# A two-layer decoder trunk on one core: a place of its own for turned weights, and a new order of the projection's pieces

## The chip, the core and the metric

The kernel runs on one core of a Trainium2 chip. The metric is the device time of one launch in microseconds, the median of several runs; lower is better. One further execution was taken by the hardware profiler, and all durations below come from it.

## What is computed

Two layers act on a residual stream x of 256 rows and 1024 columns, all in float32. Each normalises x, multiplies it with one wide input projection, runs three groups of heads, gates them and projects back:

```python
for layer in range(DEPTH):                                   # 2
    h = rms_norm(x, norm_g[layer])
    proj = jnp.einsum('btd,dc->btc', h, w_in[layer])         # 1024 -> 3584 columns
    sb_q, sb_k, sb_v, sb_g, mb_q, mb_k, mb_v, mb_g, mem_q, mem_g = jnp.split(proj, split_at, axis=-1)
    o_sb  = merge_heads(stick_breaking_attention(sb_q, sb_k, sb_v)) * silu(sb_g)      # 6 heads of 64
    o_mb  = merge_heads(moba_attention(rotary(mb_q), rotary(mb_k), mb_v)) * silu(mb_g)  # 6 heads
    m = rms_norm(mem, mem_norm_g[layer])                     # 256 memory rows
    mk, mv = jnp.split(jnp.einsum('bmd,dc->bmc', m, w_mem_kv[layer]), 2, axis=-1)
    o_mem = merge_heads(memory_attention(mem_q, mk, mv)) * silu(mem_g)                # 4 heads
    x = x + jnp.einsum('btc,cd->btd', jnp.concatenate([o_sb, o_mb, o_mem], -1), w_out[layer])
return rms_norm(x, final_norm_g)
```

With 256 rows the second group (mb) is plain causal softmax attention. The stick-breaking group (sb) replaces the softmax by a chain of log-sigmoids and a running sum over later keys.

## The kernel before

**Pieces and chunks.** The input projection is cut into pieces by head group and purpose: sb_q, sb_k, sb_v, sb_g, mb_q, mb_k, mb_v and mb_g have 384 columns, mem_q, mem_g, mk and mv 256; in layer 0 the first two are one piece, sb_qk. After them come three pieces of the output projection, wo0, wo1 (384 columns) and wo2 (256). The table `ORDER` (L45) gives the order of the pieces in each layer. A piece's weights are loaded in chunks of up to 128 x 768 floats (several of the eight k blocks side by side) into five `raw` tiles. The very first chunk is split into two halves.

**Two halves of each number.** A chunk is rounded to `hi` (ScalarE or VectorE, L395), VectorE subtracts to get `lo` (L404), and then the raw tile's next load is issued on SP's queue (`dma_chunk`, L377). Seven hi and lo pairs exist (`LEAD`). The activations are split in the same way. A product is three matmuls per k block: hi by hi, hi by lo, lo by hi. A "T" piece (queries, keys and gates; `tr_unit`, L492) comes out turned, with the weights as the stationary operand. An "N" piece (values, the rotated mb queries and keys, the output projection; `nat_unit`, L483) comes out with rows on the partitions.

**Heads.** Heads are handled in pairs. For sb, `sb_head` (L646) and `pair_sums` (L673) compute the scores, a chain of ScalarE and VectorE steps, two kinds of running sums on TensorE, and the weights `wT` (four tiles, held until the pair's product). For mb and mem, `soft_head` (L687) computes the softmax weights `w` with queries on the partitions; a condition on `turn["w"]` lets a pair start only when at most one pair before it has not been turned, the three mb pairs first and the two memory pairs behind them. These weights have to be turned before they can multiply the values. `pair_turn` (L711) does that: VectorE turns 32 x 32 blocks into a staging tile D (L723), SP writes D to a DRAM tile Z (L729), and four more SP issues read Z back into a tile F with the blocks in their places (L737). Three tiles D are there, and F is taken from the same three. `pair_task` (L745) multiplies F with the values (L775), frees F, multiplies with the gate and makes `mxhi` and `mxlo`, the output projection's input. Sb feeds its k blocks 0 to 2, mb 3 to 5, mem 6 and 7.

**The output projection** (L1057) first does k 0 to 5 of wo0 and wo1, then k 6 and 7 of both, then all of wo2. `resid_task` adds the result to x. In layer 0 `norm_task` then makes the next layer's input.

**Two activation buffers.** `Ts` (L285) has two of them, of 128 x 8 x 512. In a layer one holds the normalised rows (hT) and the other the normalised memory rows (mT); they change places from layer to layer. mT is read by mk and mv only.

**A planner writes the order.** The kernel is emitted by a list scheduler (`Sched`, L78). Every step of every task names its engine, its needs and its buffers, and has a cost by formula; the scheduler keeps a clock for each engine and emits the step that could start first, by priority among those close together. The order on each engine's queue is fixed by this. What the planner thinks of a DMA counts in it: a load is ready at the end of a byte queue `dma_t` at 380 GB/s plus 2200 ns (L326), and a trip to DRAM or back takes `DMA_LAT`, 3000 ns, plus its bytes at 300 GB/s, outside that byte queue (L731, L740).

**Start.** SP issues the first half chunk, the gain columns gc, the second half chunk and then xT blocks and chunks in turn; xT's first block is on ScalarE's queue (L426 to L433). In layer 0 the memory rows are loaded at the second piece (`MEM_AT`). Those for layer 1 are scaled into hT (L1023, L1049) when only mk or mv is left in layer 0's order, or after its last piece.

Of the kernel before, what the change touches and what calls it, by code (L numbers as in the profile page):

```python
# [7 lines left out]
F32 = mybir.dt.float32  # L8
# [8 lines left out]
D = 1024  # L17
# [22 lines left out]
X1_AT = 8  # L40
DMA_GBS = 380.0
SP_ISSUE = 450.0
DMA_LAT = 3000.0
MEM_AT = 1
ORDER = (["sb_qk", "mb_q", "sb_g", "mem_q", "mb_k", "mk", "mb_g", "sb_v", "mb_v", "mem_g", "mv"],  # L45
         ["mk", "mv", "sb_k", "mb_q", "mb_k", "sb_q", "mem_q", "sb_v", "sb_g", "mb_g", "mb_v", "mem_g"])
GATES = {"sb_g": ((0, 1, 2),), "mb_g": ((0, 1, 2),), "mem_g": ((0,), (1,))}
HOLD = 4000.0
SPARE2 = 2
# [146 lines left out]
def hybrid_trunk(ctx: ExitStack, tc: tile.TileContext, x, mem, norm_g, w_in, w_mem_kv, w_out,  # L196
# [73 lines left out]
    def sb(name, shape, dt=F32):  # L270
        return cpool.tile(shape, dt, name=name)
# [26 lines left out]
    S.res["a"] = Res([sb(f"a{i}", [128, 384]) for i in range(3)])  # L298
    S.res["w"] = Res([sb(f"w{i}", [128, 512]) for i in range(4)])
    S.res["ah"] = Res([(sb(f"ah{i}", [128, 384], FR), sb(f"al{i}", [128, 384], FR)) for i in range(2)])  # L300
    S.res["wT"] = Res([sb(f"wT{i}", [128, 384]) for i in range(4)])
    S.res["D"] = Res([sb(f"D{i}", [128, 1024]) for i in range(3)])
    dpool = ctx.enter_context(tc.tile_pool(name="turn", bufs=1, space=bass.MemoryType.DRAM))
    S.res["Z"] = Res([dpool.tile([128, 1024], F32, name=f"Z{i}") for i in range(3)])
    S.res["ga"] = Res([sb(f"ga{i}", [128, 768]) for i in range(2)])
# [12 lines left out]

    dma_t = {"t": 500.0}

    def dma(dst, src, name=None, q=None, now=0.0):
        (q or nc.sync).dma_start(dst, src)  # L322
        if q is None:
            S.T["sp"] = max(S.T["sp"], now) + SP_ISSUE
        n = _free(dst) * 4 * dst.shape[0]
        dma_t["t"] = max(dma_t["t"], now) + n / DMA_GBS  # L326
        if name:
            S.ready[name] = dma_t["t"] + 2200.0


    class Piece:
# [42 lines left out]
                chunks.append((p, kk, c, half))  # L374
    prog = {"dma": 0, "hi": 0, "lo": 0, "cur": 0}

    def dma_chunk(now=0.0):  # L377
        j = prog["dma"]
        if j >= len(chunks):
            return  # L380
        p, kk, c, w = chunks[j]
        n = len(kk)
        dma(raws[j % RAW][:, :n * w].rearrange("p (k c) -> p k c", c=w),
            p.src[:, kk[0]:kk[0] + n, c:c + w], ("raw", j), now=now)
        prog["dma"] += 1
        if j == X67_AT:
            load_xT(6, 8, now=now)
        for t, at in enumerate((X0_AT, X1_AT)):
            if j == at:
                dma(xs[:, t, :], x_r[:, t, :], ("x", t), now=now)  # L390
        if j == CST_AT:
            dma(cst, consts[:, 0:512], "cst", now=now)
            dma(S.res["w"].items[0][2][:, :256], consts[:, 512:768], "msk", now=now)
# [29 lines left out]
        for k in range(k0 + 1, k1):  # L423
            S.ready["xT", k] = S.ready["xT", k0]

    dma_chunk()  # L426
    load_xT(0, 1, nc.scalar)
    dma(gc, gcols, "gc")
    dma_chunk()
    for k in range(1, 4):  # L430
        load_xT(k, k + 1)
# [254 lines left out]

    def soft_head(l, h, kind):  # L687
        mb = kind == "mb"
        reg = [(0, 128), (128, 384)] if mb else [(0, 256), (256, 512)]
        _, (st,) = yield R("dve", alloc=["st"], need=[("qkdone", l, kind, h)])  # L690
        sc = scs.pop((l, kind, h))
        for t, (r0, r1) in enumerate(reg):
            nc.vector.tensor_reduce(st[:, t:t + 1], sc[:, r0:r1], axis=AX.X, op=OP.max, negate=True)  # L693
            S.op("dve", 1.0417 * (r1 - r0) + 65.0)
            if t == 0:
                yield R("dve")
        _, (w,) = yield R("act", alloc=["w"], cond=lambda: 5 * l + (0 if mb else 3) + h // 2 <= turn["w"] + 1)
        for t, (r0, r1) in enumerate(reg):
            act(w[:, r0:r1], sc[:, r0:r1], AF.Exp, bias=st[:, t:t + 1], accum_out=st[:, 2 + t:3 + t])
        S.free("bank", sc)  # L700
        yield R("dve")
        nc.vector.reciprocal(st[:, 0:2], st[:, 2:4])
        S.op("dve", 81.0)
        yield R("dve")
        for t, (r0, r1) in enumerate(reg):
            ts(w[:, r0:r1], w[:, r0:r1], st[:, t:t + 1])
        S.free("st", st)
        S.mark(("w", l, kind, h))
        ws[l, kind, h] = w

    def pair_turn(l, kind, c):  # L711


        n = 3 if kind == "mb" else 4
        e = 64 * n
        D = None
        for b in range(2):
            h = 2 * c + b
            _, bufs = yield R("dve", need=[("w", l, kind, h)], alloc=[] if b else ["D"])
            D = D or bufs[0]  # L720
            w = ws.pop((l, kind, h))
            o = D[:, :4 * e].rearrange("p (j m r) -> p m j r", j=4, r=32)[:, b * n:(b + 1) * n]
            nc.vector.transpose(o, w[:, :n * 128].rearrange("p (m j r) -> p m j r", j=4, r=32))  # L723
            S.op("dve", 1.0417 * n * 128 + 65.0)
            S.free("w", w)
        turn["w"] += 1
        _, (Z,) = yield R("sp", alloc=["Z"])
        Zv = Z[:, :4 * e]
        nc.sync.dma_start(Zv, D[:, :4 * e])  # L729
        S.op("sp", SP_ISSUE)  # L730
        t = S.cur.t + DMA_LAT + 512 * e * 4 / 300.0  # L731
        S.res["D"].items.append((t, None, D))
        S.ready["dump", l, kind, c] = t
        _, (F,) = yield R("sp", need=[("dump", l, kind, c)], alloc=["D"])
        Fv = F[:, :4 * e].rearrange("p (i e) -> p i e", i=4)
        for j in range(4):
            nc.sync.dma_start(Fv[32 * j:32 * j + 32],  # L737
                              Zv.rearrange("(i r) (j e) -> j r i e", i=4, j=4)[j])
            S.op("sp", SP_ISSUE)
        t = S.cur.t + DMA_LAT + 512 * e * 4 / 300.0  # L740
        S.res["Z"].items.append((t, None, Z))
        S.ready["F", l, kind, c] = t
        Fs[l, kind, c] = F

    def pair_task(l, kind, c):  # L745
# [30 lines left out]
        if kind == "sb":  # L776
            for wT in w2:
                S.free("wT", wT)
        else:
            S.free("D", F)  # L780
        S.mark(("pv", l, kind, c))
        _, (m,) = yield R("dve", need=[("g", l, k)], alloc=["ev"])
        tt(m, o[:, :256], gT[:, k, :], OP.mult)
# [132 lines left out]
    def main():  # L916
# [16 lines left out]
            scale_task(uT, ("memT", 0), 16, mT, ("mT", 0), P_M0)  # L933
            S.spawn(rows_task(3, lambda t: gb, "mem", "rm", rcm, rbm), P_RM)

        late = []

        def late_mem():
            yield R("sp", need=[("qkdone", 0, "mb", h) for h in range(6)])
# [3 lines left out]
        for l in range(DEPTH):  # L943
# [75 lines left out]
            for i, p in enumerate(ORDER[l]):  # L1019
# [13 lines left out]
                elif p in ("sb_v", "mb_v"):  # L1033
                    yield from N_piece(p, hT, hneed, lambda t, acc: evac_v(l, p, t, acc, rr_(t), 6, "rx"))
                elif p == "mem_q":
                    yield from T_piece(p, hT, 2, hneed,
                                       lambda c, acc: evac_T(l, "mem_q", c, acc, 0.125, rb, "rx"))
                elif p == "mb_q":
                    yield from N_piece(p, hT, hneed, lambda t, acc: rope_task(
                        l, "mb_q", t, acc, rr_(t, True) if l == 0 else 0.125))  # L1040
                elif p == "mb_k":
                    yield from N_piece(p, hT, hneed, lambda t, acc: rope_task(
                        l, "mb_k", t, acc, rr_(t) if l == 0 else 1.0))
                elif p in GATES:
                    yield from T_piece(p, hT, sum(map(len, GATES[p])), hneed, lambda c, acc: gate_evac(
                        l, p[:-2], c, acc, [g for g in GATES[p] if c in g][0]))

# [76 lines left out]
```

## Time and profile before

| | |
|---|---|
| median of 3 runs | 291.1 us (290.92 to 292.39) |
| the profiled execution | 292.06 us, of which the span from first to last instruction is 290.2 |
| mean granted TensorE clock | 0.990 |
| DMA | 58.94 MB, mean 203 GB/s; weight loads mostly 384 KB each, 4.3 to 4.4 us from issue to landing (median) |
| splitting the weights | VectorE's lo 101.8 us (111 instructions), ScalarE's hi 82.4 us (103) |

How to read it: an engine's row gives its busy microseconds, its share of the span and its instructions. PEld is TensorE's loading of stationary operands, beside its matmuls. Behind a row in square brackets stand the idle time of the engine just before it and what ended it. The chain of waits goes back from the last instruction, at each step to what released it. `D<-Z` is the way back of turned weights, `Z<-D` the dump. Tiles carry no buffer numbers, and in the kernel before F is one of the tiles D.

### The profile page before, as it was taken

To read this page: it belongs to the slowest core of one execution; us is meant where nothing else is said; L and a number is where in the kernel's file an instruction comes from. 1 tells how busy PE (TensorE), PEld (TensorE's weight loads), DVE (VectorE), ACT (ScalarE), POOL (GpSimd) and SP (SyncE) were. 2 spreads that over 40 slices of the span, in tenths; PEclk is the share of its full clock that TensorE was granted. 3 is DMA by queue.
4 is the path that set the end of the run, shared out by engine and by line. 5 is a ranking of instruction groups with operands and counts; after the bars stand their busy time and mean duration, and the time that the engine had idled before them with its cause. 6 is when DMAs were issued, how large, how long until landed. Compare 5 with 4: busy or idle time off the path is not lost.

```text
span 290.2 us, 5037 instructions
## 1 busy us (share of the span) xinstructions
PE 275.3 (95%) x1757; PEld 246.0 (85%) x1757; DVE 225.2 (78%) x498; ACT 187.9 (65%) x420; POOL 4.0 (1%) x10
## 2 busy tenths in 40 slices
PE   7899999999999999969999999999999999998991
PEld 4789978998898889957989899988998889887991
DVE  3858799999997999963779467549889999976272
ACT  3979699974597567830766445638969569574052
POOL 0020000000000000000000000000000000000000
PEclk9999999999999999997999999999999999999998
DMA  6998955568679674994286947441684876992003
GB/s 190 396 403 265 365 143 173 151 202 264 185 248 306 213 218 166 283 266 139 61 282 164 308 114 252 116 158 39 184 272 161 241 210 201 308 269 61 0 2 145
DMA packets 43994, 58.94 MB, mean 203 GB/s; under 512 B 3137, under 2 KB 40641, under 8 KB 43969
## 3 DMA queue, kind: packets, MB, share of 16 engines
q1 hardware_dynamic: 43392, 57.24, 63.9%
q0 software_dynamic: 288, 1.05, 1.1%
q8 instruction: 14, 0.23, 0.3%
q10 hardware_dynamic: 288, 0.33, 0.3%
q14 instruction: 12, 0.09, 0.1%
HBM read 53.10 MB, written 5.51 MB: 202 GB/s over the span
## 4 chain that ended last, share of the span: by engine, by line
PE 59%; DMA 19%; DVE 9%; ACT 5%; issue 4%; SPq 2%; DVEq 0%; ACTq 0%
PE bank L226 58%; DMA raw<-in_w_in_dram 8%; DMA D<-Z 7%; DVE lo L248 3%; DMA gb<-in_mem_dram 3%; SPq L322 2%; DMA raw<-in_w_out_dram 2%; ACT hi L242 2%; PE bank L231 1%; DVE T L252 1%; DVE D L723 1%; DVE gT L248 1%; ACT a L244 1%; ACT w L244 1%; ACT junk L244 0%
## 5 line engine op out<-in xcount | busy, mean ns | idle before, releaser
L248 DVE TENSOR_TENSOR lo<-raw,hi 128x768 fp32r<-128x768 f32 (+2 forms) x111 | 101.8, 922 | 15.4 <-ACT hi L242 14.4
L226 PE MATMUL bank<-T,hi 128*128 128x512 f32 (+1 forms) x294 | 100.8, 396 | 1.4 <-ACT hi L242 1.1
L242 ACT CAST hi<-raw 128x768 fp32r<-128x768 f32 (+2 forms) x103 | 82.4, 814 | 23.8 <-PE bank L226 9.7
L226 PE MATMUL bank<-hi,T 128*128 128x384 f32 (+1 forms) x320 | 77.8, 328 | 0.0
L226 PE MATMUL bank<-T,lo 128*128 128x256 f32 x288 | 73.0, 281 | 0.6 <-DVE lo L248 0.6
L226 PEld LDWEIGHTS bank<-T,hi 128*128 128x128 f32 x294 | 53.1, 188 | 12.5 <-ACT hi L242 1.3
L226 PEld LDWEIGHTS bank<-hi,T 128*128 128x128 f32 x320 | 55.8, 189 | 0.8 <-issue 0.5
L226 PEld LDWEIGHTS bank<-T,lo 128*128 128x128 f32 x288 | 53.2, 189 | 3.3 <-DVE lo L248 0.9
L226 PE MATMUL bank<-lo,T 128*128 128x384 f32 (+1 forms) x160 | 51.9, 324 | 0.0
L226 PE MATMUL bank<-hi,mxhi 128*128 128x384 f32 (+1 forms) x96 | 31.0, 323 | 0.0
L226 PE MATMUL bank<-hi,mxlo 128*128 128x384 f32 (+1 forms) x96 | 30.6, 319 | 0.0
L226 PE MATMUL bank<-lo,mxhi 128*128 128x384 f32 (+1 forms) x96 | 30.6, 319 | 0.0
L226 PEld LDWEIGHTS bank<-lo,T 128*128 128x128 f32 x160 | 30.1, 188 | 0.1
L244 ACT ACTIVATE junk<-xs 128x384 bf16<-128x384 f32 (+2 forms) x16 | 8.4, 522 | 21.9 <-DVE xs L248 21.1
L226 PEld LDWEIGHTS bank<-hi,mxhi 128*128 128x128 f32 x96 | 18.4, 191 | 1.3 <-issue 1.3
L226 PEld LDWEIGHTS bank<-hi,mxlo 128*128 128x128 f32 x96 | 18.3, 191 | 0.0
L226 PEld LDWEIGHTS bank<-lo,mxhi 128*128 128x128 f32 x96 | 18.3, 190 | 0.0
L244 ACT ACTIVATE w<-bank,st 128x256 f32<-128x256 f32 (+1 forms) x40 | 17.1, 448 | 0.6 <-DVE st L693 0.6
L693 DVE TENSOR_REDUCE st<-bank 128x1 f32<-128x256 f32 (+1 forms) x40 | 13.1, 376 | 3.8 <-PE bank L226 3.8
L242 ACT COPY gT<-bank 128x256 f32<-128x256 f32 x16 | 5.9, 371 | 15.4 <-PE bank L226 15.2
L244 ACT ACTIVATE ga<-ga 128x768 f32<-128x768 f32 (+1 forms) x24 | 15.3, 636 | 0.9 <-DVE ga L252 0.7
L248 DVE TENSOR_TENSOR xs<-bank,xs 128x384 f32<-128x384 f32 (+1 forms) x12 | 6.1, 512 | 12.5 <-PE bank L226 12.5
(115 smaller groups left out, 319.3 us busy)
## 6 DMA issues: line engine op xcount, KB each, us to landing
raw<-in_w_in_dram SPq DMA_DIRECT2D x71, 384.0 KB, 4.4
raw<-in_w_out_dram SPq DMA_DIRECT2D x20, 384.0 KB, 4.3
raw<-in_w_mem_kv_dram SPq DMA_DIRECT2D x8, 384.0 KB, 3.4
Z<-D SPq DMA_DIRECT2D x6, 384.0 KB, 4.5
D<-Z SPq DMA_DIRECT2D x24, 96.0 KB, 4.1
uT<-memT_dram SPq DMA_DIRECT2D x8, 256.0 KB, 5.1
Z<-D SPq DMA_DIRECT2D x4, 512.0 KB, 3.3
D<-Z SPq DMA_DIRECT2D x16, 128.0 KB, 6.7
```

The source lines that it names most:

```text
L226: nc.tensor.matmul(out, lhsT=lhsT, rhs=rhs, start=start, stop=stop, **kw)
L231: nc.tensor.transpose(out, in_, idt)
L242: nc.scalar.copy(out, in_)
L244: nc.scalar.activation(out, in_, func, **kw)
L248: nc.vector.tensor_tensor(out, a, b, op=op)
L252: nc.vector.scalar_tensor_tensor(out, a, s, b, op0=op0, op1=op1)
L322: (q or nc.sync).dma_start(dst, src)
L693: nc.vector.tensor_reduce(st[:, t:t + 1], sc[:, r0:r1], axis=AX.X, op=OP.max, negate=True)
L723: nc.vector.transpose(o, w[:, :n * 128].rearrange("p (m j r) -> p m j r", j=4, r=32))
```

## The change

- Turned weights come back into tiles of their own, F0 in layer 0 and F1 in layer 1: four places each, quarters of the layer's mT. They are given out once both mk and mv have been emitted in that layer. D has two tiles instead of three and is staging only; wT has five instead of four.
- `ORDER` is new in both layers. In layer 0 mk and mv stand fifth and sixth, mb_k second, mem_g last. In layer 1 the gates sb_g and mb_g come early, and sb_k, sb_v and mb_v are the last three.
- With it, layer 1's memory rows are scaled after the last piece of layer 0, since neither mk nor mv is the last one any more.
- The first half chunk is issued on ScalarE's queue, ahead of xT's first block; gc is the first issue of SP's queue.
- The planner's model of DMAs: loads and trips share one byte queue; runs of up to 1024 bytes count at 300 GB/s, longer ones at 380; a load's latency is 2200 ns as before, a trip's 3000.
- In `soft_head` the name `first` stands for an expression that was there before.

```diff
-DMA_LAT = 3000.0
+DMA_LAT = 2200.0
+DMA_GBS_1K = 300.0
+TRIP_LAT = 3000.0
 MEM_AT = 1
-ORDER = (["sb_qk", "mb_q", "sb_g", "mem_q", "mb_k", "mk", "mb_g", "sb_v", "mb_v", "mem_g", "mv"],
-         ["mk", "mv", "sb_k", "mb_q", "mb_k", "sb_q", "mem_q", "sb_v", "sb_g", "mb_g", "mb_v", "mem_g"])
+ORDER = (["sb_qk", "mb_k", "sb_g", "mb_q", "mk", "mv", "mem_q", "sb_v", "mb_g", "mb_v", "mem_g"],
+         ["mk", "mv", "mb_q", "mb_g", "sb_g", "sb_q", "mb_k", "mem_g", "mem_q", "sb_k", "sb_v", "mb_v"])
...
-    S.res["wT"] = Res([sb(f"wT{i}", [128, 384]) for i in range(4)])
-    S.res["D"] = Res([sb(f"D{i}", [128, 1024]) for i in range(3)])
+    S.res["wT"] = Res([sb(f"wT{i}", [128, 384]) for i in range(5)])
+    S.res["D"] = Res([sb(f"D{i}", [128, 1024]) for i in range(2)])
+    S.res["F0"], S.res["F1"] = Res([]), Res([])
...
+    def queue(nbytes, run, now):
+
+        dma_t["t"] = max(dma_t["t"], now) + nbytes / (DMA_GBS if run > 1024 else DMA_GBS_1K)
+        return dma_t["t"] + DMA_LAT
+
...
-        n = _free(dst) * 4 * dst.shape[0]
-        dma_t["t"] = max(dma_t["t"], now) + n / DMA_GBS
+        t = queue(_free(dst) * 4 * dst.shape[0], dst.shape[-1] * 4, now)
         if name:
-            S.ready[name] = dma_t["t"] + 2200.0
+            S.ready[name] = t
...
-    def dma_chunk(now=0.0):
+    def dma_chunk(now=0.0, q=None):
...
-    dma_chunk()
+    dma(gc, gcols, "gc")
+    dma_chunk(q=nc.scalar)
     load_xT(0, 1, nc.scalar)
-    dma(gc, gcols, "gc")
     dma_chunk()
...
-        t = S.cur.t + DMA_LAT + 512 * e * 4 / 300.0
+        t = queue(2048 * e, 4096, S.cur.t) + TRIP_LAT
         S.res["D"].items.append((t, None, D))
         S.ready["dump", l, kind, c] = t
-        _, (F,) = yield R("sp", need=[("dump", l, kind, c)], alloc=["D"])
+        _, (F,) = yield R("sp", need=[("dump", l, kind, c)], alloc=["F%d" % l])
...
-        t = S.cur.t + DMA_LAT + 512 * e * 4 / 300.0
+        t = queue(2048 * e, 1024, S.cur.t) + TRIP_LAT
...
-            S.free("D", F)
+            S.free("F%d" % l, F)
...
+                if {"mk", "mv"} <= set(ORDER[l][:i + 1]) and not S.res["F%d" % l].items and l not in given:
+                    given.add(l)
+                    for f in range(4):
+                        S.free("F%d" % l, mT[2][:, 2 * f:2 * f + 2, :].rearrange("p k c -> p (k c)").bitcast(F32))
```

More of the change, by code (lines that the diff above doesn't have):

```diff
@@ L383, in dma_chunk @@
         dma(raws[j % RAW][:, :n * w].rearrange("p (k c) -> p k c", c=w),
-            p.src[:, kk[0]:kk[0] + n, c:c + w], ("raw", j), now=now)
+            p.src[:, kk[0]:kk[0] + n, c:c + w], ("raw", j), q, now)
         prog["dma"] += 1
@@ L688, in soft_head @@
         mb = kind == "mb"
+        first = 0 if mb else 3
         reg = [(0, 128), (128, 384)] if mb else [(0, 256), (256, 512)]
@@ L696, in soft_head @@
                 yield R("dve")
-        _, (w,) = yield R("act", alloc=["w"], cond=lambda: 5 * l + (0 if mb else 3) + h // 2 <= turn["w"] + 1)
+        _, (w,) = yield R("act", alloc=["w"], cond=lambda: 5 * l + first + h // 2 <= turn["w"] + 1)
         for t, (r0, r1) in enumerate(reg):
@@ L934, in mem_loads @@
             S.spawn(rows_task(3, lambda t: gb, "mem", "rm", rcm, rbm), P_RM)
-        late = []
+        late, given = [], set()
         def late_mem():
@@ L1043, in main @@
                         l, "mb_k", t, acc, rr_(t) if l == 0 else 1.0))
-                elif p in GATES:
+                if {"mk", "mv"} <= set(ORDER[l][:i + 1]) and not S.res["F%d" % l].items and l not in given:
+                    given.add(l)
+                    for f in range(4):
+                        S.free("F%d" % l, mT[2][:, 2 * f:2 * f + 2, :].rearrange("p k c -> p (k c)").bitcast(F32))
+                if p in GATES:
                     yield from T_piece(p, hT, sum(map(len, GATES[p])), hneed, lambda c, acc: gate_evac(
```

## The prediction, made before the changed kernel was run

> **What bounds the kernel now.** I read the page first, then a table by stage, then TensorE's waits and the chain of waits.
>
> ```profile
> span 290.2 us, 5037 instructions
> ...
> PE 275.3 (95%) x1757; PEld 246.0 (85%) x1757; DVE 225.2 (78%) x498; ACT 187.9 (65%) x420; POOL 4.0 (1%) x10
> ...
> PE 59%; DMA 19%; DVE 9%; ACT 5%; issue 4%; SPq 2%; DVEq 0%; ACTq 0%
> ```
>
> TensorE is busy for 95% of the span and has the largest share of the chain. The change neither adds nor removes a matmul, so it can only fill the holes. The table by stage shows where these are (columns: stretch, its length, PE, PEld, DVE, ACT, POOL, granted clock, DMA share, GB/s):
>
> ```profile
> 0.00:10.00 10.00, 7.40 (x33) 4.55 (x34) 4.15 (x9) 5.06 (x8) 0.41 (x5) 1.00 0.77 242
> 10.00:30.00 20.00, 20.00 (x119) 18.38 (x119) 15.72 (x31) 17.50 (x39) 2.36 (x3) 1.00 0.96 351
> 30.00:118.00 88.00, 86.59 (x574) 76.74 (x573) 81.49 (x203) 65.39 (x159) 0.73 (x1) 1.00 0.70 220
> 118.00:147.00 29.00, 25.83 (x160) 23.93 (x160) 18.66 (x36) 13.70 (x29) 0.00 (x0) 0.94 0.70 180
> 147.00:257.00 110.00, 109.58 (x712) 98.57 (x711) 87.92 (x186) 73.28 (x158) 0.53 (x1) 1.00 0.66 203
> 257.00:284.00 27.00, 25.94 (x169) 23.84 (x168) 15.86 (x35) 11.34 (x27) 0.00 (x0) 1.00 0.23 54
> 284.00:290.20 6.20, 0.01 (x1) 0.00 (x0) 1.40 (x3) 1.62 (x5) 0.00 (x0) 0.80 0.45 169
> ```
>
> The holes are 2.60 us in the head, 0, 1.41 in layer 0's pieces, 3.17 in layer 0's output projection, 0.42 in layer 1's pieces, 1.06 in layer 1's output projection, and 6.2 in the tail, which the change does not touch. VectorE is the second load: 81.49 of 88 us (93%) in layer 0's pieces, 87.92 of 110 (80%) in layer 1's. TensorE's waits name the two holes in the middle:
>
> ```profile
> PE bank L226 <- DMA D<-Z: 4.2, 2, 3.2
> ```
>
> That is the way back of a turned weight pair, and the chain of waits in order of time shows why the first one is late:
>
> ```profile
> 106.30 0.70 DVE D L723
> ...
> 116.76 7.07 DMA D<-Z
> ...
> 123.85 7.14 DMA D<-Z
> ...
> 250.02 0.48 ACT mb_v L242
> ...
> 252.14 0.11 DVE ev L248
> ```
>
> The same on TensorE's and on SP's timeline:
>
> ```profile
> 105.04 2.17 PE L226 MATMUL bank<-D,mb_v 128*64 128x256 f32 x24
> ...
> 126.87 1.08 PE L226 MATMUL bank<-D,mv 128*64 128x256 f32 x8
> 131.12 1.98 PE L226 MATMUL bank<-D,mv 128*64 128x256 f32 x8 [3.17 <-DMA D<-Z]
> 133.03 0.69 PE L226 MATMUL bank<-hi,mxhi 128*128 128x384 f32 x1
> ...
> 134.15 0.36 PE L226 MATMUL bank<-hi,mxhi 128*128 128x384 f32 x1
> ...
> 134.71 0.33 PE L226 MATMUL bank<-hi,mxhi 128*128 128x384 f32 x1
> ...
> 262.91 1.08 PE L226 MATMUL bank<-D,mv 128*64 128x256 f32 x8 [1.06 <-DMA D<-Z]
> ```
>
> ```profile
> 109.36 0.34 SPq L729 DMA_DIRECT2D Z<-D  x1
> ...
> 113.12 0.46 SPq L729 DMA_DIRECT2D Z<-D  x1
> ...
> 115.68 1.98 SPq L737 DMA_DIRECT2D D<-Z  x4
> 118.21 2.96 SPq L322 DMA_DIRECT2D raw<-in_w_out_dram  x3
> 122.27 1.98 SPq L737 DMA_DIRECT2D D<-Z  x4
> ...
> 252.71 5.46 SPq L737 DMA_DIRECT2D D<-Z  x8
> ```
>
> The three D tiles serve twice, as staging of a dump and as the place that it comes back to. The three mb pairs hold all of them until their weights are used, at 105.04. Only then does VectorE turn the first memory head (106.30); the dumps leave at 109.36 and 113.12, the returns at 115.68 and 122.27, the second behind three weight loads, and each takes about 7.1 us to land. The plan had counted on 4.75 (its constants: 3.0 + 524,288 bytes at 300 GB/s), so it placed both memory products too early in TensorE's fixed order.
>
> **The change, part by part.** The working is against the profiled execution: 292.06 us, 1.86 of it around the span. The median of the runs is 291.1, which is 0.96 below; I carry the same difference over.
>
> *Places in the idle memory rows (F0, F1), D from three to two.* Staging no longer waits for mb_v: a D tile is held for one dump. The memory heads of layer 0 can turn as soon as their softmax is done. Five pairs share four places, so the fifth return, memory pair 1, still waits until a first mb pair is used. Call the end of mb_v M. The mb products take 2.17 us (105.04), the issue 1.98, the landing 7.14: with a microsecond of hand-overs the pair is there at about M + 12. It is needed after mem_g, the mb products and those steps of wo0 and wo1 that use no memory head, which are 72 matmuls (two blocks, two row halves, six k, three products). Their rate stands in this stretch of the first of them:
>
> ```profile
> 117.90:126.80 8.90, 8.90 (x53) 8.72 (x51) 7.02 (x12) 5.05 (x9) 0.00 (x0) 1.00 1.09 272
> ```
>
> That is 0.168 us each: 12.1 for the 72, 8.1 for a piece of 48, and, since mem_g has two thirds of such a piece's columns, 5.4 for it. So the pair is needed at M + 5.4 + 2.2 + 12.1 = M + 19.7 in layer 0: 7.7 us of cover. The hole goes whole, and with it the slow restart. The products after the wait took 1.98 instead of 1.08, and the three matmuls from 133.03 took 1.12 against 0.56 for the three from 134.15: 0.90 + 0.56. Gain 3.17 + 0.90 + 0.56 = 4.6. Least gain, if the memory chain moves up by half only: 1.5.
>
> The restart is a matter of the clock: the row for 118 to 147 has a granted 0.94, and the pause of 1.06 at 262.91 left the products at 1.08. The Trainium skill (TensorE: Matmul & The Clock Gate, Part 1: The HAM clock gate) says that the clock halves after an idle window of about 3.4 us and needs as long to come back; an estimate by that page is half of 3.4, 1.7 lost, so 4.9 for this term and a sum of -5.5 below. The trace shows 1.46 lost after a pause of 3.17, so a pause just under the page's window was enough.
>
> *Layer 1's return.* There mb_v is now the last piece, so the fifth pair is there at M + 12 and needed at M + 2.2 + 12.1 = M + 14.3: 2.3 us of cover. Before, both memory returns were issued after 252.71 and cost 1.06. The trip is now planned in the same byte queue as the loads, so the product should be placed later. I take -0.7, between -1.06 (gone) and what rival 1 says.
>
> *mb_v last in layer 1.* From its copy (250.02) to the first product with the gate (252.14) are 2.1 us, and the hi and lo parts follow; 3.2 in all is my estimate. TensorE has the three sb steps of wo0 (9 matmuls, 1.5 us) and the mb products (2.2) meanwhile. +0.3, between 0 and 1.7 (3.2 less the 1.5).
>
> *Memory k, v early; new order.* The matmuls are the same. In layer 0 mk comes 5.4 us sooner (mem_q no longer stands ahead of it) and mv five pieces sooner, and both need the scaled memory rows and their statistics from a VectorE that is 93% busy; the work for layer 1's memory rows moves from before the last piece into the output projection, where VectorE has 18.66 of 29 us. In layer 1 the sb heads move to the end and two gates to the front. VectorE and ScalarE have the same total; layer 1 stood at 80% with 0.42 us lost, layer 0 at 93% with 1.41 lost, so a denser last third is worth about the difference of these, 1 us, at most. I take +0.2, near to nothing, because the totals are unchanged; it lies between -1.8 (1.41 and 0.42 both gone) and rival 2.
>
> *First half chunk on ScalarE's queue.*
>
> ```profile
> 0.74 0.38 SPq L322 DMA_DIRECT2D raw<-in_w_in_dram  x1
> 0.76 0.39 ACTq L322 DMA_DIRECT2D uT<-xT_dram  x1
> ...
> 1.18 0.42 SPq L322 DMA_DIRECT2D gc<-gcols_dram  x1
> ...
> 4.07 0.51 ACT L244 ACTIVATE T<-uT,gc 128x256 fp32r<-128x256 f32 x1 [2.06 <-DMA gc<-gcols_dram]
> ...
> 7.45 0.83 ACT L242 CAST hi<-raw 128x768 fp32r<-128x768 f32 x1 [0.61 <-DMA raw<-in_w_in_dram]
> ...
> 8.33 1.66 PE L226 MATMUL bank<-T,hi 128*128 128x512 f32 x6 [1.14 <-ACT hi L242]
> ```
>
> Each SP issue after the first goes out 0.44 us sooner (1.18 - 0.74). The xT column behind the chunk on ScalarE's queue goes 0.39 later, while gc, for which the first step waited at 4.07, comes 0.44 sooner: the first matmul may slip by up to 0.3. But TensorE waits again at 8.33 for a cast that waited for its chunk, and from there on it is full. So the head is worth what that chunk gains: -0.4, between -0.44 and +0.3.
>
> *The rest* (a fifth wT, the loads at 300 GB/s for short rows): 0. It alters the plan only; matmuls, casts and bytes are the same.
>
> Sum: -0.4 - 4.6 - 0.7 + 0.3 + 0.2 = -5.2. That is 286.9 us for a profiled execution and 291.1 - 5.2 = 285.9 as a median.
>
> **The rivals.**
>
> *1. The fifth pair stalls layer 1 instead.* Its cover is thin (2.3 us), SP's queue put three loads ahead of the second return, and the plan's error for one landing was 2.4 (7.14 against 4.75). If the return again stands behind such loads (from 117.66, where the first four issues end, to 122.27: 4.6 us), the hole is 4.6 - 2.3 = 2.3, and the restart adds between nothing (as after 1.06) and 1.46 (as after 3.17), say 0.8: 3.1 us more than forecast, 289.0. Against it: the weight loads are nearly all out by then (23% DMA share from 257 on).
>
> *2. Layer 1's end is bound by the sb chain: slower.*
>
> ```profile
> 212.90 0.92 PE L226 MATMUL bank<-sb_q,sb_k 64*128 64x256 f32 x8
> ...
> 228.58 0.87 PE L226 MATMUL bank<-wT,sb_v 128*64 128x256 f32 x8
> ```
>
> The last sb pair took 15.7 us from its scores to its product, when the memory and mb softmax shared VectorE. Now it has sb_v and mb_v behind it, 16.2 us, and its result is the first that wo0 uses. More is queued on VectorE then, six sb heads and four memory heads at once. If the chain takes 22.5 us, TensorE stands for 6.3, and the restart adds 1.5: 7.8 less 5.2 is +2.6, 293.7. It makes the kernel slower by over 0.5% from a chain of about 21.4 us on (16.2 + 5.2, with the 1.5 of the restart as the excess). For it: 93% load in layer 0. Against: layer 0 lost only 1.41 at that load.
>
> *3. What goes at the end comes back in layer 0.* mk and mv finish before the memory rows' statistics are there, their four accumulators keep four of the eight banks, and the heads' scores wait for banks. If the 1.41 grows by 4.5, the change is worth -0.7: 290.4. Against it: the mb scores start sooner too, and the third sb pair has a fifth wT.
>
> **How the numbers follow.** Forecast 0.58, rival 1 0.16, rival 3 0.12, rival 2 0.14. Half a per cent is 1.5 us, about what a measurement of this kernel can tell from no change. Faster: the forecast and three quarters of rival 1, 0.70. Same: the rest of rival 1 and most of rival 3, 0.14. Slower: rival 2 and the tail of rival 3, 0.16. The forecast's own bounds are -0.44 - 4.63 - 1.06 + 0 - 1.8 = -7.9 (283.2) and about -1.5 (289.6); with the spread of the runs the low end is 282.6. The high end takes in rivals 1 and 3 and the milder half of rival 2: 292.6.
>
> **What would show it.** Layer 0's output projection without a wait for D<-Z and at clock 1.00, about 24.4 us long instead of 29; memory dumps that leave before the mb products; the matmul of 8.33 near 7.9; a wait of under 0.5 us on the return in layer 1; VectorE at about 85% to 93% in layer 1's last third with TensorE full. A wait of TensorE for mxhi or wT before wo0 in layer 1 would speak for rival 2, one of over 2 us on the return for rival 1, PE idle of over 4 us between 40 and 100 for rival 3. I am wrong if TensorE's holes outside head and tail still sum to 5 us or more.

## The result, and the profile after

The changed kernel takes 282.95 us (282.13 to 284.54 in six runs), the kernel before 291.4 beside it (289.12 to 292.39 in six): a ratio of 0.9719 [0.9675, 0.9763], 8.45 us off where 5.2 were forecast. The forecast's side and range hold; the gain is 1.6 times the forecast, and much of this document is about those 3 us. A ratio here and below compares undisturbed runs alone, so it is not always the quotient of the two medians beside it.

The page of the changed kernel, its span, its load and the chain of waits by engine:

```profile
span 280.5 us, 5046 instructions
...
PE 271.7 (97%) x1757; PEld 245.7 (88%) x1757; DVE 225.0 (80%) x496; ACT 189.8 (68%) x422; POOL 3.9 (1%) x10
...
PE 92%; DMA 3%; DVE 1%; ACT 1%; issue 1%; ACTq 0%
```

The DMA share of the chain fell from 19% to 3%. The span is 9.7 us shorter (290.2 to 280.5): TensorE's idle time fell by 6.1 us (14.9 to 8.8), its busy time by 3.6 for the same 1757 matmuls. Part of that 3.6 is the slow restart of 1.46 (matmuls that ran at half clock behind the hole). The rest is probably pauses too: the profile models the ends of matmuls, so short pauses can hide in them. That is argued, not shown.

The table by stage (columns as in the prediction's) has the same four stretches, moved to where they now begin:

```profile
10.00:114.50 104.50, 104.50 (x684) 94.23 (x684) 96.33 (x227) 81.60 (x186) 2.97 (x4) 1.00 0.82 265
114.50:139.40 24.90, 24.90 (x161) 23.30 (x161) 18.71 (x41) 15.93 (x39) 0.00 (x0) 1.00 0.55 150
139.40:244.70 105.30, 104.78 (x670) 95.06 (x669) 84.50 (x176) 75.27 (x163) 0.53 (x1) 1.00 0.67 205
244.70:274.30 29.60, 29.57 (x210) 27.84 (x208) 19.27 (x43) 9.85 (x23) 0.00 (x0) 1.00 0.24 73
```

The stretch of layer 0's output projection was 29.00 us long with TensorE busy for 25.83 at a granted clock of 0.94; it is now 24.90 long, full, at 1.00. After the head the whole kernel has one hole left. All of TensorE's waits (us in total, times, longest):

```profile
PE bank L228 <- DVE junk L927: 1.2, 1, 1.2
PE bank L228 <- ACT T L246: 0.9, 1, 0.9
PE bank L233 <- DVE w L254: 0.5, 1, 0.5
```

No return of turned weights is among them. TensorE's timeline shows where the memory products (`mv`) now stand, and in the row of 144.05 the hole of 0.52 us (the last row is the last matmul):

```profile
5.24 1.14 PE L228 MATMUL bank<-T,hi 128*128 128x256 f32 x6 [0.88 <-ACT T L246]
...
7.64 1.62 PE L228 MATMUL bank<-T,hi 128*128 128x512 f32 x6
...
107.77 2.17 PE L228 MATMUL bank<-T,mb_v 128*64 128x256 f32 x24
...
114.56 0.34 PE L228 MATMUL bank<-hi,mxhi 128*128 128x384 f32 x1
...
116.76 1.08 PE L228 MATMUL bank<-T,mv 128*64 128x256 f32 x8
...
125.78 1.08 PE L228 MATMUL bank<-T,mv 128*64 128x256 f32 x8
...
139.41 0.40 PE L228 MATMUL bank<-T,hi 128*128 128x512 f32 x1
...
144.05 0.66 PE L233 MATMUL bank<-cst,w 128*128 128x128 f32 x4 [0.52 <-DVE w L254]
...
260.48 1.08 PE L228 MATMUL bank<-T,mv 128*64 128x256 f32 x8
...
273.99 0.28 PE L228 MATMUL bank<-lo,mxhi 128*128 128x256 f32 x1
```

Both products of layer 0 take 1.08, where the late one had taken 1.98. On SP's queue, around them:

```profile
96.10 0.38 SPq L737 DMA_DIRECT2D Z<-D  x1
...
103.28 1.83 SPq L745 DMA_DIRECT2D T<-Z  x4
...
105.86 0.47 SPq L737 DMA_DIRECT2D Z<-D  x1
107.17 8.99 SPq L330 DMA_DIRECT2D raw<-in_w_out_dram  x6
116.25 1.84 SPq L745 DMA_DIRECT2D T<-Z  x4
```

Both memory dumps (96.10, 105.86) leave before the mb products at 107.77, as the places allow; before, they left at 109.36 and 113.12, after them. The first return leaves at 103.28 instead of 115.68. The second still leaves late, at 116.25, behind six weight loads (the fence's 8.99 us), because its place was an mb pair's until 107.77; its product is 9.5 us behind it, so nothing waits.

For comparing kernels the span is cut in three: up to the first full-width step (the head), from there to layer 1's first matmul (layer 0), and from there to the end of the last matmul (layer 1). What follows, the tail, is 6.2 us in both. The two rows of before that this needs beside its 8.33:

```profile
147.22 0.40 PE L226 MATMUL bank<-T,hi 128*128 128x512 f32 x1
...
283.73 0.28 PE L226 MATMUL bank<-lo,mxhi 128*128 128x256 f32 x1
```

| kernel | head | layer 0 | layer 1 | span |
|---|---|---|---|---|
| before | 8.33 | 138.89 | 136.79 | 290.2 |
| after | 7.64 | 131.77 | 134.86 | 280.5 |
| gain | 0.69 | 7.12 | 1.93 | 9.7 |

The gain of 9.7 in the profiled executions is 8.45 in the medians, because the one of before (292.06) lies 0.66 above its median and the one of after (282.32) 0.63 below its own.

### The profile page after: what moved, and what is told of

It is laid out like the page before. It is cut to its first block, busy times and chain, and to the rows that moved or that the text cites. A ratio compares the mean times of both kernels' runs of the same rounds, so it can differ in the third digit from the quotient of the medians.

```text
span 280.5 us, 5046 instructions
## 1 busy us (share of the span) xinstructions
PE 271.7 (97%) x1757; PEld 245.7 (88%) x1757; DVE 225.0 (80%) x496; ACT 189.8 (68%) x422; POOL 3.9 (1%) x10
## 4 chain that ended last, share of the span: by engine, by line
PE 92%; DMA 3%; DVE 1%; ACT 1%; issue 1%; ACTq 0%
PE bank L228 90%; DMA raw<-in_w_in_dram 2%; PE bank L233 1%; DMA uT<-xT_dram 1%; DVE lo L250 1%; DVE xs L250 0%; ACT junk L246 0%; DVE w L254 0%; ACT xs L246 0%; ACT ss L246 0%; ACT T L246 0%; ACT T L244 0%; ACT L205 0%; DVE ss L514 0%; ACT hi L244 0%
## 5 line engine op out<-in xcount | busy, mean ns | idle before, releaser
L244 ACT CAST hi<-raw 128x768 fp32r<-128x768 f32 (+2 forms) x106 | 84.2, 812 | 13.2 <-PE bank L228 5.8
L246 ACT ACTIVATE T<-uT,gc 128x256 fp32r<-128x256 f32 x24 | 11.3, 500 | 2.7 <-DMA uT<-xT_dram 2.7
```

Source lines behind the costliest of these rows:

```text
L244: nc.scalar.copy(out, in_)
L246: nc.scalar.activation(out, in_, func, **kw)
```

## The experiments

The kernel before differs from run to run and from one set of runs to the next: its median was 291.4 beside the changed kernel and 290.93, 289.51 and 289.2 beside the experiments, where its single runs lay between 285.3 and 294.3. The changed kernel's spread is 2.4 us, and it was not timed again beside the experiments. So the kernels below are read by their ratio, their own median and above all by their holes and stages, against the changed kernel. All of them plan the order of the instructions anew, on every engine, which is itself part of what they show.

**The places** (the changed kernel with the returns going to three shared D tiles again, and four wT):

```diff
...
-    S.res["D"] = Res([sb(f"D{i}", [128, 1024]) for i in range(2)])
...
+    S.res["D"] = Res([sb(f"D{i}", [128, 1024]) for i in range(3)])
...
-        _, (F,) = yield R("sp", need=[("dump", l, kind, c)], alloc=["F%d" % l])
+        _, (F,) = yield R("sp", need=[("dump", l, kind, c)], alloc=["D"])
...
-            S.free("F%d" % l, F)
+            S.free("D", F)
...
```

> The changed kernel with the turned weights coming back into the D tiles again (three D, four wT, no F places); order, head and planner stay new. Theory 1, the places made the gain: the memory heads turn only after the mb products, so with mb_v's end as M the second pair lands at about M + 26 (105.04 to 130.99 in the kernel before), while it is needed at M + 19.7 in layer 0 and M + 14.3 in layer 1: holes of about 6 and 12 us and two slow restarts of 1.5, so about 283 + 21 = 304 us, and at least 295. Theory 2, the order alone made it: 283 to 285 us.

Measured: 291.07 us, ratio 0.9996 [0.9964, 1.0029]; the whole gain is gone. TensorE's timeline, then SP's:

```profile
109.65 2.24 PE L228 MATMUL bank<-D,mb_v 128*64 128x256 f32 x24
...
134.53 3.68 PE L228 MATMUL bank<-D,mv 128*64 128x256 f32 x16 [5.37 <-DMA D<-Z]
138.14 0.69 PE L228 MATMUL bank<-hi,mxhi 128*128 128x384 f32 x1
```

```profile
116.04 0.34 SPq L736 DMA_DIRECT2D Z<-D  x1
...
118.10 0.34 SPq L736 DMA_DIRECT2D Z<-D  x1
...
127.25 5.22 SPq L744 DMA_DIRECT2D D<-Z  x8
```

The mechanism of the prediction is there as it was told: without places the dumps leave only after the mb products (116.04 and 118.10 behind 109.65), the returns at 127.25, and TensorE stands for 5.37 us. The 16 products after it take 3.68 us where two groups of eight at 1.08 would be 2.16, and the matmuls behind them start slowly too (0.69 for the first): the restart costs about 2.3 (see the end). Hole and restart, 7.7 us, are nearly all of the 7.85 that layer 0 takes longer than in the changed kernel (139.62 against 131.77). Both theories missed the time. The hole of layer 0 came nearly as expected (6 us), but layer 1, where 12 us and a second restart were expected, has none. This profiled execution is the longest of its ten, 292.19, at a granted clock of 0.95 nearly throughout (0.938 in the mean, 0.981 to 0.990 in the other nine), so its stages are rather too long.

**The order** (the changed kernel with the old list of pieces in both layers):

```diff
-ORDER = (["sb_qk", "mb_k", "sb_g", "mb_q", "mk", "mv", "mem_q", "sb_v", "mb_g", "mb_v", "mem_g"],
-         ["mk", "mv", "mb_q", "mb_g", "sb_g", "sb_q", "mb_k", "mem_g", "mem_q", "sb_k", "sb_v", "mb_v"])
+ORDER = (["sb_qk", "mb_q", "sb_g", "mem_q", "mb_k", "mk", "mb_g", "sb_v", "mb_v", "mem_g", "mv"],
+         ["mk", "mv", "sb_k", "mb_q", "mb_k", "sb_q", "mem_q", "sb_v", "sb_g", "mb_g", "mb_v", "mem_g"])
```

> The changed kernel with the old ORDER. The places of layer 0 are given out only when mv, its last piece, is done, so all five returns leave after that. Theory 1 in the form 'places need mk and mv early': mb's three pairs are needed at the fourth k step of wo0, at about 1.5 us, and land after 3 x 2 us of issues and 5 to 7 us: a hole of 9 us or more in layer 0, none in layer 1: about 283 + 10 = 293 us. Theory 2: the old order gives the old time, 289 to 292. Theory 3, places alone suffice: 283 to 285.

Measured: 296.67 us, ratio 1.0191 [1.0149, 1.0234]. Slower than both. SP's timeline and TensorE's:

```profile
114.81 1.90 SPq L745 DMA_DIRECT2D T<-Z  x4
```

```profile
120.53 1.55 PE L228 MATMUL bank<-T,mb_v 128*64 128x256 f32 x8 [4.90 <-DMA T<-Z]
```

The places are given out once mk and mv are both emitted, and the old list has mv last: no pair of layer 0 can come back before the pieces are over. TensorE's waits in layer 0 sum to 8.0 us, 5.5 of them for returns, and half clock behind them adds some 3.7. The new order of layer 0 is therefore no edit beside the places but the one that lets them be given out.

**Layer 1's order alone** (the old list in layer 1 only, the second line of the diff above):

> The changed kernel with the old ORDER in layer 1 only. If the new order of layer 1 matters by itself, its hole of 1.06 us (wait for the return beside mem_g, the old last piece) or another one comes back: 284 to 286. If places and plan are what layer 1 needed: 283.

Measured: 284.47 us, ratio 0.9875 [0.9798, 0.9952]. Layer 0 is 131.69, as in the changed kernel; layer 1 is 135.51 against 134.86. TensorE's only wait after the head is the one that the changed kernel has too:

```profile
PE bank L233 <- DVE w L254: 0.7, 1, 0.7
```

So layer 1's list is worth some 0.7 us by its stage, and it is the first list, not the second, that carries the change. The medians are 1.5 apart; in the profiled executions the rest of the difference is in the head, 9.13 against 7.64, which varies by itself.

**The new order without the rest** (the kernel before with both new lists):

```diff
-ORDER = (["sb_qk", "mb_q", "sb_g", "mem_q", "mb_k", "mk", "mb_g", "sb_v", "mb_v", "mem_g", "mv"],
+ORDER = (["sb_qk", "mb_k", "sb_g", "mb_q", "mk", "mv", "mem_q", "sb_v", "mb_g", "mb_v", "mem_g"],
...
```

> The kernel before with only the new ORDER. Theory 1: the same holes as with shared places, 295 to 304 us, slower than before. Theory 2: nearly the whole gain, 283 to 286 us.

Measured: 292.35 us, ratio 1.0087 [1.0045, 1.0128]: slightly slower, not faster, and neither of the theories' times. Its waits have the old hole, cut in two:

```profile
PE bank L226 <- DMA D<-Z: 2.9, 2, 1.7
```

The profiled execution is the shortest of the ten, 290.02, with a mean granted clock of 0.998. Eight of the others have 0.978 to 0.989 and take 291.81 to 294.37. A stretch of 3.4 us at half clock, as behind the hole of before, takes 0.006 off the mean (half of 3.4 in 290), so the other runs probably paid for a restart that this profile does not show. That is an estimate, since they have no trace.

**The planner's old view of DMAs** (the changed kernel, with the loads' rate and the trips' times as they were):

```diff
-DMA_GBS_1K = 300.0
+DMA_GBS_1K = 380.0
...
-        t = queue(2048 * e, 4096, S.cur.t) + TRIP_LAT
+        t = S.cur.t + TRIP_LAT + 512 * e * 4 / 300.0
...
-        t = queue(2048 * e, 1024, S.cur.t) + TRIP_LAT
+        t = S.cur.t + TRIP_LAT + 512 * e * 4 / 300.0
```

> The changed kernel with the planner's old view of DMAs: 380 GB/s for every load, trips outside the byte queue. Theory 1: the pairs have cover enough, so the plan's error of some 2 us in a landing does not show: within 1 us of 283. Rival, the better plan made the gain: a wait for D<-Z returns, 1 to 5 us, 284 to 288.

Measured: 290.31 us, ratio 0.9972 [0.994, 1.0004]. The same matmuls, the same bytes, the same places and lists, and 7.4 us of the changed kernel's 8.45 are gone, more than either theory allowed. TensorE's waits, its timeline and SP's:

```profile
PE bank L228 <- DMA T<-Z: 2.6, 2, 2.4
PE bank L228 <- ACT mxhi L244: 1.2, 1, 1.2
...
PE bank L228 <- ACT mb_v L246: 1.1, 1, 1.1
```

```profile
122.48 1.21 PE L228 MATMUL bank<-T,mv 128*64 128x256 f32 x8 [2.42 <-DMA T<-Z]
123.62 0.69 PE L228 MATMUL bank<-hi,mxhi 128*128 128x384 f32 x1
...
259.11 0.45 PE L228 MATMUL bank<-hi,mxhi 128*128 128x384 f32 x1 [1.22 <-ACT mxhi L244]
```

```profile
110.03 4.03 SPq L330 DMA_DIRECT2D raw<-in_w_out_dram  x3
114.15 2.94 SPq L745 DMA_DIRECT2D T<-Z  x4
```

The return of 114.15 stands behind three loads, its product is placed where the old view thinks it has landed, and TensorE waits 2.42 us for it at 122.48: the old hole, in a kernel that has the places. The matmul right after takes 0.69 where such a one takes 0.34: from 123.31 the granted clock is 0.50 for 3.41 us, which costs about 1.7. Together 4.1 of the 6.5 us that layer 0 takes longer than in the changed kernel; four smaller waits, 1.08 of them for mb_v, make up 1.8 more.

**Only the trips as before** (the last two lines of that diff, the loads at 300):

> The changed kernel with the trips planned as before (outside the byte queue, 3.0 us and the bytes: 4.75 for a memory pair's return), but short-row loads at 300 GB/s as new. The plan's view of DMAs was worth about 7 us (the run with all of it old, 290.3 against 283). Theory A, the trips: their planned 4.75 against a landing of up to 7.1 puts the last memory product too early in TensorE's order: a hole of 2.4 and a restart in layer 0, and 287 to 291 us. Theory B, the loads' rate: it is new here, so 283.

Measured: 286.79 us, ratio 0.9979 [0.9927, 1.003]. No wait for a return at all, so the mechanism that was expected of it, a hole at the trip, did not come. Layer 0 is 132.27, nearly the changed kernel's; the loss is in layer 1, 139.60 against 134.86. Of these 4.74 the waits name 2.2 in two rows, and 0.3 more for mxlo. A microsecond behind these the granted clock is 0.50 for 3.41 us (the second view below, columns as in the prediction's table), with TensorE full, which costs about 1.7 more:

```profile
232.79 0.92 PE L228 MATMUL bank<-sb_q,sb_k 64*128 64x256 f32 x6 [1.01 <-ACT w L246]
...
254.43 0.45 PE L228 MATMUL bank<-hi,mxhi 128*128 128x384 f32 x1 [1.23 <-ACT mxhi L244]
```

```profile
256.58:259.99 3.41, 3.41 (x12) 3.41 (x11) 0.00 (x0) 0.37 (x1) 0.00 (x0) 0.50 0.51 143
```

In layer 0 the trip is planned at 4.75 as in the kernel before, and yet its last product does not wait:

```profile
112.31 1.75 SPq L745 DMA_DIRECT2D T<-Z  x4
```

```profile
118.97 1.08 PE L228 MATMUL bank<-T,mv 128*64 128x256 f32 x8
```

The two kernels with the old trips differ in the loads' rate alone. At 300 the return leaves 1.8 us sooner than at 380 (112.31 against 114.15), and its product stands 6.7 us behind it, where at 380 TensorE was ready 5.9 us behind it (122.48 - 2.42 - 114.15). So with the places and the new list it is the loads' rate in the plan that closes layer 0's hole, theory B's part, and the trips' time costs in layer 1, by waits that are not for a return.

**A longer trip, outside the byte queue** (as the one before, with the constant at 5200):

```diff
-TRIP_LAT = 3000.0
+TRIP_LAT = 5200.0
```

> The changed kernel with the trips planned outside the byte queue but with the latency that the changed kernel's code adds up to, 2.2 + 3.0 = 5.2 us (6.95 for a memory pair's return, against 7.1 measured in the kernel before). Theory A1, the longer latency alone moves the products late enough: 283 to 284. Theory A2, the shared byte queue is needed, since trips collide with loads: the wait for the return stays in part, 285 to 290.

Measured: 285.68 us, ratio 0.9917 [0.9862, 0.9973]. It is theory A2's time, but not its wait: none is for a return. Layer 0 is 131.64, layer 1 is 137.14, with one wait of over half a microsecond after the head:

```profile
233.58 0.92 PE L228 MATMUL bank<-sb_q,sb_k 64*128 64x256 f32 x6 [1.04 <-ACT w L246]
```

**The new view of DMAs without the rest** (the kernel before, with `queue`, its constants and the trip lines of the change):

```diff
-DMA_LAT = 3000.0
+DMA_LAT = 2200.0
+DMA_GBS_1K = 300.0
+TRIP_LAT = 3000.0
...
-        t = S.cur.t + DMA_LAT + 512 * e * 4 / 300.0
+        t = queue(2048 * e, 4096, S.cur.t) + TRIP_LAT
...
```

> The kernel before with only the new view of DMAs in the planner; order, shared D tiles and head old. If the right landing times are enough by themselves, the plan puts the 3.3 us of independent output projection work ahead of the second memory product and most of the holes of 3.17 and 1.06 us close: 285 to 287. If shared tiles and the old order hold the memory pairs back whatever the plan knows: within 1 us of before, 289 to 291.

Measured: 288.42 us, ratio 1.0001 [0.9959, 1.0042]: no gain by the ratio, 1.1 us by the medians (289.51 beside it). Its waits have no return either, but another row:

```profile
PE bank L228 <- DVE mxhi L265: 3.4, 4, 0.9
```

The plan now knows that the returns come late and puts the memory products later, right ahead of the matmuls that use their result (`mxhi`), four of which then wait 0.85 each. Without the places the better plan traded one wait for another.

Side by side, sorted by what was undone (in us; the head left out, since it varies by itself, see the end):

| kernel | layer 0 | layer 1 | profiled execution | median |
|---|---|---|---|---|
| after | 131.77 | 134.86 | 282.32 | 282.95 |
| old order | 144.74 | 135.35 | 297.24 | 296.67 |
| shared places | 139.62 | 135.38 | 292.19 | 291.07 |
| planner's old view | 138.29 | 136.85 | 290.79 | 290.31 |
| trips as before, loads new | 132.27 | 139.60 | 287.53 | 286.79 |
| longer trip outside the queue | 131.64 | 137.14 | 285.70 | 285.68 |
| old order in layer 1 only | 131.69 | 135.51 | 284.39 | 284.47 |
| before, new order alone | 136.64 | 136.88 | 290.02 | 292.35 |
| before, new view alone | 134.45 | 137.64 | 288.23 | 288.42 |
| before | 138.89 | 136.79 | 292.06 | 291.4 |

In layer 0 the changed kernel's relatives fall into two groups: about 132 with the places, the new list and the loads counted at 300, and 138 to 145 where one of these is undone. The two relatives of the kernel before lie between, 134 and 137; that is one profiled execution of each against one of before at 292.06, and their medians lie 1.4 above and 1.1 below before's beside them. In layer 1, where the prediction saw 0.7 us, it is the trips' planned time that shows: 139.60, 137.14 and 134.86 as it goes from 3.0 to 5.2 us of latency and into the byte queue, 1.7 of the first step being the half clock.

**The small edits.** Three kernels undo the rest of the list, one at a time: the old head, a head with gc on ScalarE's queue, and four wT tiles:

```diff
-    dma(gc, gcols, "gc")
-    dma_chunk(q=nc.scalar)
+    dma_chunk()
     load_xT(0, 1, nc.scalar)
+    dma(gc, gcols, "gc")
     dma_chunk()
```

> The changed kernel with the old head: first half chunk, gc, second half chunk on SP, xT's first block alone on ScalarE's queue. From the two profiles: the first matmul returns to 4.63 (from 5.24), but the first one of the second k step goes from 7.64 back to 8.33, and TensorE is full from there: +0.7 us, 283.6. Rival, bytes bind the head and the queue does not matter: no difference, 283.

```diff
-    dma(gc, gcols, "gc")
-    dma_chunk(q=nc.scalar)
+    dma_chunk()
     load_xT(0, 1, nc.scalar)
+    dma(gc, gcols, "gc", nc.scalar)
     dma_chunk()
```

> The changed kernel with the first half chunk first on SP and gc behind xT's first block on ScalarE's queue: every later SP issue as early as in the changed kernel, xT's block as early as in the kernel before. If the issue time is what counts: first matmul near 4.6 and second k step at 7.6 or a little before: 0 to 0.6 us faster than 283, 282.4 to 283. If gc, now the second one of its queue, comes later than 4.1, the first matmul slips and nothing is gained: 283.

```diff
-    S.res["wT"] = Res([sb(f"wT{i}", [128, 384]) for i in range(5)])
+    S.res["wT"] = Res([sb(f"wT{i}", [128, 384]) for i in range(4)])
```

> The changed kernel with four wT tiles instead of five. If the fifth tile took away the wait of the first sb product for its values and the heads' waits in layer 0 (about 1 us of the 1.41 us in the pieces): +0.5 to +1.5, 283.5 to 284.5. If these went with the order: no difference, 283.

Measured: 282.69 (ratio 0.979 [0.975, 0.983]), 282.6 (0.9787 [0.9743, 0.9832]) and 283.14 us (0.9803 [0.9757, 0.9849]), against 282.95. By their ratios they would stand about 2 us behind the changed kernel (0.9719), but that was timed beside other runs of before, and the stages do not show it: layer 0 takes 132.25, 131.76 and 131.85 us, layer 1 134.25, 134.35 and 134.23 (the changed kernel 131.77 and 134.86). So neither the head nor the fifth wT is worth anything that can be told here.

**Three places instead of four:**

```diff
-                    for f in range(4):
+                    for f in range(3):
```

> The changed kernel with three return places in each layer instead of four, so that both memory pairs wait for an mb product. With mb_v's end as M, the two returns land at about M + 3 + 2 x 2 + 7 = M + 14; needed at M + 19.7 in layer 0 (cover holds) and at M + 14.3 in layer 1 (just): theory 1 expects 0 to 2 us more, 283 to 285. If the places were no limit at all, no difference; if the fourth place is what keeps the memory pairs out of each other's way, a wait of 3 us and a restart come back in layer 1: 287.

Measured: 283.81 us (283.1 to 284.18), ratio 0.9828 [0.9776, 0.9879], with no wait for a return in either layer. At most some 0.9 us for the fourth place, and the interval overlaps with those of the three kernels above, which were timed against the same runs: two returns have to wait for an mb pair instead of one, and the plan puts their products late enough (261.06 for a return at 250.14 in layer 1).

The last four kernels are plans drawn anew as well, and all lie between 282.6 and 283.8. So a new plan alone need not scatter the time by several microseconds, and the 3.8 to 13.7 us by which the old trips, the old view, the shared places and the old order lie above the changed kernel are more than that. The 2.7 of the longer trip and the 1.5 of layer 1's list are nearer to it.

## Why the prediction was right, and where it failed

**Right.** The bound (holes of TensorE, no work removed), the biggest hole, and its cause. The output projection of layer 0 was to take 24.4 us and takes 24.85 (139.41 - 114.56) after 29.29, a gain of 4.4 for the 4.6 of the sum; the dumps leave before the mb products; the clock stays at 1.00. Layer 1's return cost 1.06 and costs nothing, the better end of the -0.7. mb_v as the last piece, +0.3 in the sum, shows no wait. VectorE in layer 1's last third is at 96% with TensorE full (33.34 of 34.70 us from 210 on), a little above the 85% to 93% that were named. The head's -0.4 is 0.69 in the two profiles but nothing in the medians.

**Failed: "The rest ... 0. It alters the plan only."** In this kernel the plan is the product: every engine runs a fixed order, and where the plan has a landing too early, an engine waits. The prediction had the evidence and used it: it blamed the hole on a plan that "had counted on 4.75" for a landing of 7.14. Then it put the loads' rate at nothing and gave the trips' lines a part in layer 1's 0.7 only. The planner's old view in an otherwise unchanged kernel costs 7.4 us; in the stages, the loads' rate is worth 6.0 us of layer 0 (138.29 against 132.27) and the trips' lines 0.5 of layer 0 and 4.7 of layer 1. (These do not add up: with the old trips, the new rate makes layer 1 longer, 139.60 against 136.85.) The part ahead of the prediction also read the new lines too shortly: `queue` adds its own 2200 ns ahead of the trip's 3000, so a trip is planned at 5.2 us and its bytes, 6.95 for a memory pair, instead of 4.75. That is as much as the 7.07 and 7.14 of before, but more than most returns need now: the pieces of the memory pairs' returns land after 4.9 us in the median, in the kernel before after 6.7. The new figure leaves room; it is not simply a better measurement.

**Failed: the order's "+0.2".** It was called near to nothing "because the totals are unchanged", with -1.8 as the better end, since only 1.83 us of idle time were seen in the pieces. Up to layer 0's output projection the kernel gained 3.4 us (117.93 to 114.56), 0.7 of it in the head, so the pieces 2.7; layer 1 gained 0.9 besides its return. That is 3.6 where 1.83 us of holes were shown, so the better end failed as well: the busy time of the profile, with its modelled ends, was no floor here. Nor is the gain the order's alone: up to the output projection layer 0 takes 109.60 us before and 106.92 after, 107.33 with the order alone and 107.20 with the planner's new view alone.

**Failed: the hole's credit.** The 4.6 were given to the places alone. Without the places it is gone, but without the new order, or with the planner's old view, it is gone too; and the order alone gains nothing, the view alone 1.1 us at most. The terms were added as if they were independent; layer 0's three edits are one edit.

**The rivals.** Rival 1 (the fifth pair stalls layer 1) and rival 3 (the loss returns among the pieces of layer 0) are not seen; the fifth return leaves late as rival 1 said, but its product is planned for that. Rival 2, the slower one, has its place right and its price wrong: with the planner's old view or the old trips, wo0's products in layer 1 wait for mxhi, 1.22 and 1.23 us instead of 6.3, once with a restart behind it.

**Open.** Some 0.6 us of layer 0 in the planner's old view, and 0.5 of layer 1 with the old trips (1.0, since the changed kernel's own wait of 0.52 is missing there), which neither a wait nor the clock names. The loads at 380 with the new trips were not run, and neither was the old order with places that need not wait for mk and mv, so whether places of another kind would do without the new list is not shown. Each kernel is one plan with one profile.

## What to carry to other kernels

Where a planner or a hand-written order sets the queues, a measured landing that differs from the planned one can be a hole by itself: compare each transfer's time from issue to landing with what the plan counts on, and price a change of those constants like a change of the code. Ask of several edits to one stage whether one is the condition of another before adding their gains; here the order alone and the view alone gained at most 1.1 us, and with the places layer 0 gained 7. Read a gain by stages that begin and end at the same matmul, since the holes seen in the pieces of one profile missed half of what was gained there. And look at the granted clock behind each pause of over a microsecond, since a restart can cost more than the pause.

## What the runs showed of the hardware that was not expected

**The first matmuls.** Their duration has two values. TensorE's timelines of the kernel with four wT tiles and of the one with the old head:

```profile
5.00 1.65 PE L228 MATMUL bank<-T,hi 128*128 128x256 f32 x6 [0.65 <-ACT T L246]
...
9.01 1.30 PE L228 MATMUL bank<-T,hi 128*128 128x512 f32 x4
```

```profile
4.61 1.65 PE L228 MATMUL bank<-T,hi 128*128 128x256 f32 x6 [0.26 <-ACT T L246]
...
8.04 1.65 PE L228 MATMUL bank<-T,hi 128*128 128x512 f32 x6
```

The first six take 1.65 us here and 1.14 in the changed kernel's profile (5.24), though the instructions and the head's DMAs of the kernel with four wT are the same, and the clock column has 1.00 for the first 10 us of before and after alike. The first full-width step comes at 7.64 or at 9.01 by that. Over all profiled kernels the new head has it at 7.6 to 7.7 in three and at 8.9 to 9.2 in six, the old head at 8.0 to 8.5 in four, the one with gc on ScalarE's queue at 9.1. So the head's 0.69 us of the profiles is the luck of two executions, as the medians say.

**The restart.** It is no fixed price. In each profile in which the clock falls before the last matmul, it is granted at 0.50 for a stretch of 3.41 us or two or three times that; just ahead of it and behind it the column has 1.00 (0.95 with the shared places). From the kernel before, the old view, the shared places and the old order, with the bounds read off finer slices:

```profile
130.77:134.18 3.41, 3.06 (x12) 2.01 (x13) 1.91 (x6) 0.00 (x0) 0.00 (x0) 0.50 0.80 272
```

```profile
123.31:126.72 3.41, 3.41 (x14) 3.10 (x11) 2.78 (x8) 0.83 (x3) 0.00 (x0) 0.50 0.40 130
```

```profile
132.33:139.18 6.85, 4.65 (x19) 2.90 (x20) 2.01 (x6) 0.00 (x0) 0.00 (x0) 0.50 0.26 60
```

```profile
119.04:129.28 10.24, 7.32 (x31) 4.37 (x31) 4.48 (x11) 0.00 (x0) 0.00 (x0) 0.50 0.88 296
```

Half of the busy time in these stretches is an estimate of the price: 1.5 us after a pause of 3.17 (1.46 by the matmuls), 1.7 after one of 2.42, 2.3 after one of 5.37, 3.7 after one of 4.90 with further waits behind it, and 1.7 in the kernel with the old trips after waits of 1.23 and 0.32. The pause of 1.06 had none, nor had those of 1.70 and 1.24 in the profiled execution of the order alone. So the length of the pause alone does not tell whether the clock falls. In the old view it falls at 123.31, when TensorE has been working again for 0.8 us. The Trainium skill (TensorE: Matmul & The Clock Gate, Part 1: The HAM clock gate) gives an idle window of about 3.4 us; the traces agree with that length in the stretches of 3.41 us, and differ on the pause, which need not fill a window: 2.42 was enough.
